# A channel mixer's memory in two pools, one of them aligned to 512 bytes, and a more urgent weight split

## The chip, the cores and the metric

The kernel runs on one core of one Trainium2 chip. The metric is the device time of one execution in microseconds (us); of several executions the median is taken. A core has a matrix engine (TensorE, PE in the profile; its weight loads are PEld), a vector engine (VectorE, DVE), a scalar engine (ScalarE, ACT), a general one (GpSimd, POOL) and a queue that issues transfers (SyncE, SP). They run side by side, each through its own list of instructions in a fixed order, and wait for each other by semaphores. They work on an on-chip memory of 128 partitions; addresses below are bytes within a partition.

## The reference

A trunk of two layers over x of 512 tokens by 1024 channels, in float32. Each layer has a token mixer and then a channel mixer, each between two RMS norms. Layer 0's token mixer is retention beside neighbourhood attention, layer 1's a bidirectional state-space scan. The channel mixer, which the change is about, is the same in both:

```python
h = rms_norm(x, g_pre)
u = depthwise_conv_centered(h @ w_up, conv_w, conv_b)   # width 3 along the tokens
g, v = split(u)                                          # 2816 channels each
x = x + rms_norm((gelu(g) * v) @ w_down, g_post)
```

## The kernel before

**Products in three parts.** A float32 operand is split into a high part (a cast, on ACT) and a low part (source less high part, on DVE): `Env.split`, lines 107 and 108. A product is then three matmuls, high by high, high by low and low by high: `Env.mm3`, lines 116 to 118. So each weight tile goes through a load (`wst`, on SP's queue), a cast to `whi` on ACT, a subtraction to `wlo` on DVE, and then TensorE.

**The channel mixer, up stage** (`ffn`). The normed tokens come in four tiles t0 to t3. Each is scaled (`xs`, line 164), turned by eight transposes (`pt`, line 173) and split into `xh`, `xl`. Weights come in units of 1024 columns. The first four units are applied to the first 256 tokens, before the last two token tiles are turned, and then to the other 256 (128x256 matmuls). Units one and two lie in `whi`/`wlo`. Units three and four lie in tiles that serve something else later: unit three as `xb1h`, `xb1l` (where the down stage's `b1h`, `b1l` will be) and unit four as `xe2` (which the profile prints as `xe`). In layer 1, whose first two units are loaded while mixer 1 still runs, the casts of units three and four are told to stand behind the second cast of token tile 1 (`behind`). The other units follow at 512 columns, then the convolution (line 398 on ACT, 399 and 400 on DVE) and the gated product `H`.

**The down stage** (`down_strassen`) forms the second product by Strassen's scheme in seven products, with sums of quarters of the weight prepared in DRAM. Its moving operands are weights, its stationary ones parts of `H`: even products take them from `b1h`, `b1l` (`ab1h`, `ab1l` in the profile), odd ones from the memory of `xh`, `xl` (`axh`, `axl`). Weights are split in `weights`; in the last product, units 4 and 5 are split into `x1` (memory of `s3`) and `x2` (memory of `e2`). Between the products stand the post-norms of token tiles (`k`, `v_m`, `x`), and the next layer's `xs`.

**What sets the order.** A scheduler lays the instructions of each engine in the order of the program, except that work inside `tc.high_priority(n)` counts as n steps more urgent and can pass other work. It also lays tiles into memory. A pool of tiles that takes space of pools that are closed has to wait, at its first write, for all that used that space. Before, the channel mixer has one pool, `ffn_c`, at 123904 to 228032. In it lie `cwt` (the convolution's weights, 704 bytes), then `H`, `b1h`, `b1l`, `e2`, `s3`, then `wx` and the `k` tiles; behind the 704 bytes each of these starts 192 bytes past a multiple of 512. In layer 1 its space covers that of mixer 1's last tiles, `e` and `m` (218624 to 228864).

Of the kernel before, what the change touches and what calls it, by code (L numbers as in the profile page):

```python
# [8 lines left out]
F32 = mybir.dt.float32  # L9
R32 = mybir.dt.float32r  # L10
# [7 lines left out]
P = 128  # L18
S = 512
# [255 lines left out]
    return out  # L275


def down_strassen(E, pool, w, ts, H, first, g_post, done):

    nc, tc = E.nc, E.tc
    lower, upper = slice(0, HW), slice(HW, S)
    A11, A21 = H[:, :HK, upper], H[:, :HK, lower]
    A12, A22 = H[:, HK:, upper], H[:, HK:, lower]
    k0 = [0]

    def stage(i, u, cols):
        st = pool.tile([P, 1024], F32, name="wx") if k0[0] % 4 == 3 else E.wst.tile([P, 1024], F32, name="wst")
        k0[0] += 1  # L290
        nc.sync.dma_start(st[:, :cols], quarters(*i)[u])
        return st[:, :cols]

    def weights(i, u, extra=None):
        cols = 1024 if u < HK // 2 else 512
        st = stage(i, u, cols)
        if extra is None:
            hi, lo = E.whi.tile([P, 1024], R32, name="whi"), E.wlo.tile([P, 1024], R32, name="wlo")
        else:
            hi, lo = extra[:, :1024], extra[:, 1024:]  # L300
        with tc.high_priority(60):
            E.split(hi[:, :cols], lo[:, :cols], st)
        return [(hi[:, c:c + 512], lo[:, c:c + 512]) for c in range(0, cols, 512)]

    a, bb = ([E.mm.tile([P, 512], F32, name="mm") for _ in range(2)] for _ in range(2))
    s3 = pool.tile([P, HK, HW], F32, name="s3")
    d = []

    def raw(i):
        tt, stt = nc.vector.tensor_tensor, nc.vector.scalar_tensor_tensor  # L310
        if i == 1:
            tt(s3, A11, A21, op=ALU.subtract)
            return s3
        if i == 2:
            tt(A21, A22, A21, op=ALU.subtract)
            stt(A11, A11, -1.0, A21, op0=ALU.mult, op1=ALU.subtract)
            return A11
        if i == 6:
            stt(A11, A12, -1.0, A11, op0=ALU.mult, op1=ALU.subtract)
            return A11  # L320
        return {3: A22, 4: A21, 5: A12}[i]

    def prepare(i):
        if i % 2:
            hi, lo = (E.res.tile([P, HK, HW], R32, name="a" + n, tag=n) for n in ("xh", "xl"))
        else:
            hi, lo = (pool.tile([P, HK, HW], R32, name="a" + n, tag=n) for n in ("b1h", "b1l"))
        src = raw(i)
        for c in (slice(0, 5), slice(5, HK)):
            E.split(hi[:, c], lo[:, c], src[:, c])  # L330
        return hi, lo

    seq = ((w, 0), a), ((ts, 1), bb), ((ts, 2), a), ((ts, 3), bb), ((ts, 0), a), ((w, 2), d), ((w, 3), a)
    kept = {}
    st = {}
    op, nxt = first, None
    started = []
    for i, (src, bank) in enumerate(seq):
        last = i == len(seq) - 1
        if not bank:  # L340
            bank.extend(E.px.tile([P, 512], F32, name="pd", tag="px") for _ in range(2))
        more = any(bank is x for x in started)
        started.append(bank)

        def mms(t, ws, u):
            for j, w_ in enumerate(ws):
                k = 2 * u + j
                cc = slice(t * P, t * P + P)
                E.mm3(bank[t], op[0][:, k, cc], op[1][:, k, cc], *w_, not more and k == 0, k == HK - 1, more)

        if last:
            ex = {4: pool.tile([P, 2048], R32, name="x1", tag="s3"), 5: pool.tile([P, 2048], R32, name="x2", tag="e2")}
            ws = [weights(src, u, ex.get(u)) for u in range(HK // 2 + 1)]
            for t in range(2):
                for u, x in enumerate(ws):
                    if (t, u) == (0, 1):
                        E.operands()
                    if u == 1:
                        E.finish(f"t{t}", st, done)
                    mms(t, x, u)  # L360
                E.post_half(st, 2 + t, 1, bank[t], g_post, sign=-1.0)
                E.finish(f"x{2 + t} s{2 + t}", st, done)
            continue
        for uu in ((0,), (1,), (2,), (3,), (4, 5)):
            ws = [(weights(src, u), u) for u in uu]
            for t in range(2):
                for x, u in ws:
                    mms(t, x, u)
            if uu == (1,):
                nxt = prepare(i + 1)  # L370
        op = nxt
        for t in range(2):
            if i in (0, 1, 2):
                kept[i, t] = pool.tile([P, 512], F32, name=f"k{i}{t}")
                nc.scalar.copy(kept[i, t], bank[t])
            else:
                j, tok, n = {3: (2, 0, 0), 4: (1, 0, 1), 5: (0, 2, 0)}[i]
                m = kept[j, t]
                nc.vector.tensor_tensor(m, bank[t], m, op=ALU.add)
                E.post_half(st, tok + t, n, m, g_post, m=m, sign=1.0 - 2 * n)  # L380
                if i == 4:
                    E.finish(f"x{t} s{t}", st, done)
    E.late += [lambda s=s: E.finish(s, st, done) for s in LATE]


def ffn(E, w_up, cw, w_down, ts, g_post_row, done, w1=None):


    nc, tc = E.nc, E.tc
    with ExitStack() as ctx:  # L390
        cp = ctx.enter_context(tc.tile_pool(name="ffn_c", bufs=1))
        cwt = cp.tile([P, 2, NF, 4], F32, name="cwt")
        H = cp.tile([P, NF, S], F32, name="H")

        def conv(ps, s, f):
            w = lambda i: cwt[:, s, f, i:i + 1]
            o = E.tmp.tile([P, S], F32, name=f"cv{s}", tag="tmp")
            nc.scalar.activation(o, ps, AF.Identity, scale=w(1), bias=w(3))  # L398
            nc.vector.scalar_tensor_tensor(o[:, 1:], ps[:, :S - 1], w(0), o[:, 1:], op0=ALU.mult, op1=ALU.add)  # L399
            nc.vector.scalar_tensor_tensor(o[:, :S - 1], ps[:, 1:], w(2), o[:, :S - 1], op0=ALU.mult, op1=ALU.add)  # L400
            return o

        def tail(f, pg, pv):
            g = conv(pg, 0, f)
            nc.scalar.activation(g, g, AF.Gelu_apprx_tanh)  # L405
            v = conv(pv, 1, f)
            nc.vector.tensor_tensor(H[:, f], g, v, op=ALU.mult)

        def extra(tags):
            t = [cp.tile([P, 2048 // len(tags)], R32, name="x" + n, tag=n) for n in tags]  # L410
            t = t if len(t) == 2 else [t[0][:, :1024], t[0][:, 1024:]]
            return [x[:, c:c + 512] for x in t for c in (0, 512)]

        u0, u1, st = w1 or (E.wunit(w_up[0, 0]), E.wunit(w_up[1, 0]), None)

        behind = E.turned[1][1] if w1 else None
        w0 = [[u0, u1], [E.wunit(w_up[0, 1], extra(("b1h", "b1l")), st, behind=behind),
                         E.wunit(w_up[1, 1], extra(("e2",)), behind=behind)]]
        nc.sync.dma_start(cwt, cw)
        p0 = [[E.mm.tile([P, S], F32, name="mm") for s in range(2)] for f in range(2)]  # L420
        for c in range(2):
            for i in range(4):
                f, s = i // 2, i % 2
                E.proj_fm(p0[f][s], w0[f][s], c * 256, c * 256 + 256)
                if c == 0 and i in (1, 2):
                    E.flush()
        for f in range(2):
            tail(f, *p0[f])
        for f in range(2, NF):
            ps = []  # L430
            for s in range(2):
                behind = w1 and f == 2
                st = E.wload(w_up[s, f], E.mid if behind and s == 0 else None)
                w = E.wunit(None, st=st, behind=E.turned[3][1] if behind else None)
                ps.append(E.mm.tile([P, S], F32, name="mm"))
                E.proj_fm(ps[-1], w)
            tail(f, *ps)
            E.chore(2)
            if f == HK + 3:
                first = [cp.tile([P, HK, HW], R32, name="a" + n, tag=n) for n in ("b1h", "b1l")]  # L440
                for k in range(0, HK, 4):
                    c = slice(k, min(k + 4, HK))
                    E.split(first[0][:, c], first[1][:, c], H[:, c, HW:])
        g_post = E.bcast(g_post_row)
        down_strassen(E, cp, w_down, ts, H, first, g_post, done)


def log1p_exp_neg(E, alloc, z):
# [884 lines left out]
```

## Time and profile before

| | |
|---|---|
| median of three runs | 1391.11 us (1390.11 to 1395.13) |
| profiled execution, its own time | 1389.62 us |
| its span | 1387.8 us |
| mean granted TensorE clock | 0.997 |

The profile is of one execution. Times in its rows are us from the start of the span, and 1.8 us lie around the span. In it layer 0's channel mixer lasts from 262 to 623 us (its down stage from 470), mixer 1 to 1026, and layer 1's channel mixer to the end. A row of the timeline gives start, duration, engine, line, operation, output and inputs; what stands in brackets is the idle time before the instruction and who ended it. A name after the arrow is an input: of a matmul first the moving operand, then the stationary one.

### The profile page before, as it was taken

What the parts mean: (1) busy time and instruction counts of PE and PEld (TensorE: products, weight loads), DVE (VectorE), ACT (ScalarE), POOL (GpSimd) and SP (SyncE); (2) the same over time, 40 slices, a digit from 0 to 9 for tenths busy, and PEclk for the clock granted to TensorE, in tenths of its full rate; (3) what the DMA queues carried; (4) which work ended last, traced back from release to release, by engine and by line L of the source; (5) the groups of instructions that cost most, each with busy time, mean ns of one, the idle gap of its engine ahead of it and who ended that gap; (6) DMA issues with size and microseconds to landing.
All of it is one profiled execution on the core that took longest, in us unless ns stands there. A gap on an engine that the chain in (4) does not pass through costs nothing.

```text
span 1387.8 us, 18078 instructions
## 1 busy us (share of the span) xinstructions
PE 1358.7 (98%) x6776; PEld 1119.8 (81%) x6776; DVE 984.4 (71%) x1402; ACT 758.2 (55%) x1233; POOL 108.9 (8%) x130
## 2 busy tenths in 40 slices
PE   7999999999999999999999999999989999999997
PEld 6877777898888888888778787777879888888886
DVE  7378888655565559797878686897886556556876
ACT  5356666443433345564978787377454434334563
POOL 0011110100011100010000010000010001110000
PEclk9999999999999999999999999999999999999999
DMA  7443232246679926653565454273434668993654
GB/s 294 146 139 107 88 90 96 69 143 238 230 204 231 227 85 198 195 190 127 159 184 181 137 183 141 68 204 117 140 126 160 218 223 225 225 221 97 196 180 142
DMA packets 69368, 229.81 MB, mean 166 GB/s; under 512 B 8352, under 2 KB 9120, under 8 KB 68768
## 3 DMA queue, kind: packets, MB, share of 16 engines
q1 hardware_dynamic: 54224, 167.30, 37.3%
q0 software_dynamic: 7168, 46.14, 13.7%
q10 hardware_dynamic: 7888, 15.21, 4.1%
q8 instruction: 54, 0.88, 0.3%
q14 instruction: 34, 0.28, 0.1%
HBM read 221.01 MB, written 51.64 MB: 196 GB/s over the span
## 4 chain that ended last, share of the span: by engine, by line
PE 85%; ACT 5%; DVE 4%; DMA 2%; issue 2%; POOL 1%; DVEq 0%; SPq 0%; POOLq 0%; ACTq 0%
PE mm L116 25%; PE mm L117 25%; PE mm L118 25%; PE pi L999 1%; PE st L948 1%; ACT pb L978 1%; DMA pb<-pd 1%; PE py L1019 1%; DMA wst<-in_c_fm 1%; PE pt L173 1%; ACT whi L107 1%; DVE wlo L108 1%; PE y L674 1%; PE pt L892 1%; PE pd L118 0%
## 5 line engine op out<-in xcount | busy, mean ns | idle before, releaser
L116 PE MATMUL mm<-xh,whi 128*128 128x512 f32 (+1 forms) x1216 | 464.0, 382 | 0.7 <-ACT z L918 0.3
L117 PE MATMUL mm<-xh,wlo 128*128 128x512 f32 (+2 forms) x1216 | 462.9, 381 | 1.1 <-DVE wlo L108 1.1
L118 PE MATMUL mm<-xl,whi 128*128 128x512 f32 (+2 forms) x1216 | 463.3, 381 | 0.5 <-DVE xl L108 0.5
L108 DVE TENSOR_TENSOR wlo<-wst,whi 128x1024 fp32r<-128x1024 f32 (+1 forms) x232 | 279.6, 1209 | 65.5 <-ACT whi L107 64.8
L107 ACT CAST whi<-wst 128x1024 fp32r<-128x1024 f32 (+1 forms) x232 | 238.4, 1032 | 102.4 <-PE mm L117 67.9
L116 PEld LDWEIGHTS mm<-xh,whi 128*128 128x128 f32 x1216 | 228.2, 188 | 45.9 <-issue 2.5
L118 PEld LDWEIGHTS mm<-xl,whi 128*128 128x128 f32 (+1 forms) x1216 | 228.0, 188 | 45.0 <-issue 1.3
L117 PEld LDWEIGHTS mm<-xh,wlo 128*128 128x128 f32 (+1 forms) x1216 | 228.3, 188 | 44.1 <-DVE wlo L108 1.5
L399 DVE SCALAR_TENSOR_TENSOR cv<-mm,cwt,cv 128x511 f32<-128x511 f32 x88 | 65.9, 749 | 182.4 <-ACT cv L398 182.4
L398 ACT ACTIVATE cv<-mm,cwt 128x512 f32<-128x512 f32 x88 | 68.6, 780 | 212.7 <-PE mm L118 212.7
L978 ACT ACTIVATE pb<-pb,tok 128x128 f32<-128x128 f32 x256 | 80.8, 392 | 8.7 <-DMA pb<-pd 7.3
L400 DVE SCALAR_TENSOR_TENSOR cv<-mm,cwt,cv 128x511 f32<-128x511 f32 x88 | 66.0, 750 | 2.8
L117 PE MATMUL mm<-whi,ab1l 128*128 128x512 f32 x164 | 64.5, 393 | 0.0
L116 PE MATMUL mm<-whi,ab1h 128*128 128x512 f32 x164 | 64.5, 393 | 0.0
L118 PE MATMUL mm<-wlo,ab1h 128*128 128x512 f32 x164 | 63.7, 389 | 0.0
L912 DVE SCALAR_TENSOR_TENSOR xf<-mm,cwt,xf 128x511 f32<-128x511 f32 (+1 forms) x64 | 47.5, 743 | 6.9 <-ACT xf L909 6.4
L274 POOL DMA_DIRECT2D ts<-in_f_down x48 | 29.9, 647 | 272.2 <-PE mm L118 267.7
L405 ACT ACTIVATE cv<-cv 128x512 f32<-128x512 f32 x44 | 27.8, 633 | 42.3 <-DVE cv L400 42.2
L116 PE MATMUL mm<-whi,yh 128*128 128x512 f32 x104 | 40.9, 395 | 1.7 <-DVE xf L912 1.7
L117 PE MATMUL mm<-whi,yl 128*128 128x512 f32 x104 | 41.1, 395 | 0.0
L1031 POOL TENSOR_TENSOR sq<-sq 128x512 f32<-128x512 f32 x11 | 16.7, 1514 | 309.9 <-ACT sq L1025 246.3
L118 PE MATMUL mm<-wlo,yh 128*128 128x512 f32 x104 | 40.6, 391 | 0.0
(308 smaller groups left out, 2120.7 us busy)
## 6 DMA issues: line engine op xcount, KB each, us to landing
wst<-in_f_up SPq DMA_DIRECT2D x88, 512.0 KB
ts<-in_f_down POOLq DMA_DIRECT2D x48, 704.0 KB, 5.8
wst<-in_c_fm SPq DMA_DIRECT2D x40, 512.0 KB
wst<-ts SPq DMA_DIRECT2D x32, 512.0 KB
pb<-pd ACTq DMA_DIRECT2D x29, 512.0 KB
wst<-in_f_down SPq DMA_DIRECT2D x24, 512.0 KB
ts<-ts POOLq DMA_DIRECT2D x16, 704.0 KB, 9.3
wst<-in_ab_fm SPq DMA_DIRECT2D x20, 512.0 KB
```

Of the source, the lines that this page charges most:

```text
L107: first = self.nc.scalar.copy(hi, src)
L108: second = self.nc.vector.tensor_tensor(lo, src, hi.bitcast(F32), op=ALU.subtract)
L116: mm(out, lh, rh, start=first, stop=False)
L117: mm(out, ll, rh, start=False, stop=False)
L118: self.product = mm(out, lh, rl, start=False, stop=last)
L274: out.append(lambda i=i, src=src, j=j, c=c, kw=kw: gp.dma_start(part(ts, i, c), part(src, j, c), **kw))
L398: nc.scalar.activation(o, ps, AF.Identity, scale=w(1), bias=w(3))
L399: nc.vector.scalar_tensor_tensor(o[:, 1:], ps[:, :S - 1], w(0), o[:, 1:], op0=ALU.mult, op1=ALU.add)
L400: nc.vector.scalar_tensor_tensor(o[:, :S - 1], ps[:, 1:], w(2), o[:, :S - 1], op0=ALU.mult, op1=ALU.add)
L405: nc.scalar.activation(g, g, AF.Gelu_apprx_tanh)
L912: nc.vector.scalar_tensor_tensor(r[:, a], ps[:, b], wc(j), r[:, a], op0=ALU.mult, op1=ALU.add)
L978: nc.scalar.activation(pb[:, dr, c], pb[:, dr, c], AF.Identity, scale=1.0 - 2 * dr, bias=tok[:, 0, c, dr * H + h:dr * H + h + 1])
```

## The change

It does three things. (1) The pool is made two: `ffn_h` holds `H`, `b1h`, `b1l`, `e2` and `s3` from 123904 to 210944, each now at a multiple of 512; `ffn_c` holds `cwt` at 210944, and `wx` and the `k` tiles where they were. The sum of both is as large as before. (2) `s3` is made in `ffn` and handed to `down_strassen`. (3) The weight splits of the down stage are made urgent by 150 steps in place of 60.

```diff
--- before.py
+++ after.py
@@ -275,7 +275,7 @@
     return out
 
 
-def down_strassen(E, pool, w, ts, H, first, g_post, done):
+def down_strassen(E, big, pool, w, ts, H, s3, first, g_post, done):
 
 
 
@@ -298,12 +298,11 @@
             hi, lo = E.whi.tile([P, 1024], R32, name="whi"), E.wlo.tile([P, 1024], R32, name="wlo")
         else:
             hi, lo = extra[:, :1024], extra[:, 1024:]
-        with tc.high_priority(60):
+        with tc.high_priority(150):
             E.split(hi[:, :cols], lo[:, :cols], st)
         return [(hi[:, c:c + 512], lo[:, c:c + 512]) for c in range(0, cols, 512)]
 
     a, bb = ([E.mm.tile([P, 512], F32, name="mm") for _ in range(2)] for _ in range(2))
-    s3 = pool.tile([P, HK, HW], F32, name="s3")
     d = []
 
     def raw(i):
@@ -324,7 +323,7 @@
         if i % 2:
             hi, lo = (E.res.tile([P, HK, HW], R32, name="a" + n, tag=n) for n in ("xh", "xl"))
         else:
-            hi, lo = (pool.tile([P, HK, HW], R32, name="a" + n, tag=n) for n in ("b1h", "b1l"))
+            hi, lo = (big.tile([P, HK, HW], R32, name="a" + n, tag=n) for n in ("b1h", "b1l"))
         src = raw(i)
         for c in (slice(0, 5), slice(5, HK)):
             E.split(hi[:, c], lo[:, c], src[:, c])
@@ -349,7 +348,7 @@
                 E.mm3(bank[t], op[0][:, k, cc], op[1][:, k, cc], *w_, not more and k == 0, k == HK - 1, more)
 
         if last:
-            ex = {4: pool.tile([P, 2048], R32, name="x1", tag="s3"), 5: pool.tile([P, 2048], R32, name="x2", tag="e2")}
+            ex = {4: big.tile([P, 2048], R32, name="x1", tag="s3"), 5: big.tile([P, 2048], R32, name="x2", tag="e2")}
             ws = [weights(src, u, ex.get(u)) for u in range(HK // 2 + 1)]
             for t in range(2):
                 for u, x in enumerate(ws):
@@ -388,9 +387,8 @@
 
     nc, tc = E.nc, E.tc
     with ExitStack() as ctx:
-        cp = ctx.enter_context(tc.tile_pool(name="ffn_c", bufs=1))
-        cwt = cp.tile([P, 2, NF, 4], F32, name="cwt")
-        H = cp.tile([P, NF, S], F32, name="H")
+        hp, cp = (ctx.enter_context(tc.tile_pool(name=n, bufs=1)) for n in ("ffn_h", "ffn_c"))
+        H = hp.tile([P, NF, S], F32, name="H")
 
         def conv(ps, s, f):
             w = lambda i: cwt[:, s, f, i:i + 1]
@@ -407,7 +405,7 @@
             nc.vector.tensor_tensor(H[:, f], g, v, op=ALU.mult)
 
         def extra(tags):
-            t = [cp.tile([P, 2048 // len(tags)], R32, name="x" + n, tag=n) for n in tags]
+            t = [hp.tile([P, 2048 // len(tags)], R32, name="x" + n, tag=n) for n in tags]
             t = t if len(t) == 2 else [t[0][:, :1024], t[0][:, 1024:]]
             return [x[:, c:c + 512] for x in t for c in (0, 512)]
 
@@ -416,6 +414,8 @@
         behind = E.turned[1][1] if w1 else None
         w0 = [[u0, u1], [E.wunit(w_up[0, 1], extra(("b1h", "b1l")), st, behind=behind),
                          E.wunit(w_up[1, 1], extra(("e2",)), behind=behind)]]
+        s3 = hp.tile([P, HK, HW], F32, name="s3")
+        cwt = cp.tile([P, 2, NF, 4], F32, name="cwt")
         nc.sync.dma_start(cwt, cw)
         p0 = [[E.mm.tile([P, S], F32, name="mm") for s in range(2)] for f in range(2)]
         for c in range(2):
@@ -437,12 +437,12 @@
             tail(f, *ps)
             E.chore(2)
             if f == HK + 3:
-                first = [cp.tile([P, HK, HW], R32, name="a" + n, tag=n) for n in ("b1h", "b1l")]
+                first = [hp.tile([P, HK, HW], R32, name="a" + n, tag=n) for n in ("b1h", "b1l")]
                 for k in range(0, HK, 4):
                     c = slice(k, min(k + 4, HK))
                     E.split(first[0][:, c], first[1][:, c], H[:, c, HW:])
         g_post = E.bcast(g_post_row)
-        down_strassen(E, cp, w_down, ts, H, first, g_post, done)
+        down_strassen(E, hp, cp, w_down, ts, H, s3, first, g_post, done)
 
 
 def log1p_exp_neg(E, alloc, z):
```

The built programs differ in these places. On ACT, at the start of layer 1's channel mixer (`xh<-pt` turns token tiles, `ssx` and `ssm` are sums of squares for the norms, `m` is a tile of mixer 1; in brackets the engines and queues that a row waits for), before:

```order
L107 CAST xh<-pt 128x4x128 [waits PE_49] x2
L153 ACTIVATE junk,ssx<-x 128x1025 [waits DVE_49,Activation_49]
L153 ACTIVATE junk,ssm_8963<-m 128x512 [waits Activation_49]
L153 ACTIVATE junk,ssm_8983<-m 128x512 [waits DVE_49,Activation_49]
L107 CAST xh<-pt 128x4x128 [waits PE_49]
L107 CAST xb1h<-wst 128x512 [waits DVE_49,DMAHW2_49,Activation_49,Pool_49]
L107 CAST xb1h<-wst 128x512
L153 ACTIVATE junk,ssx<-x 128x1025 [waits DVE_49]
L107 CAST xe_9034<-wst 128x512 [waits DMAHW4_49]
L107 CAST xe_9034<-wst 128x512
L107 CAST xh<-pt 128x4x128 [waits PE_49] x3
```

and now:

```order
L107 CAST xh<-pt 128x4x128 [waits PE_49] x2
L107 CAST xb1h<-wst 128x512 [waits DMAHW2_49,Activation_49,Pool_49]
L107 CAST xb1h<-wst 128x512
L107 CAST xe_9040<-wst 128x512 [waits DMAHW4_49]
L107 CAST xe_9040<-wst 128x512
L153 ACTIVATE junk,ssx<-x 128x1025 [waits DVE_49]
L153 ACTIVATE junk,ssm_8967<-m 128x512 [waits Activation_49]
L153 ACTIVATE junk,ssm_8987<-m 128x512 [waits DVE_49,Activation_49]
L107 CAST xh<-pt 128x4x128 [waits PE_49] x2
L153 ACTIVATE junk,ssx<-x 128x1025 [waits DVE_49,Activation_49]
L107 CAST xh<-pt 128x4x128 [waits PE_49] x2
```

The casts of `xb1h` and `xe` now stand right behind the two casts of token tile 1, ahead of the sums of squares of tile 2, and the first of them no longer waits for DVE.

On TensorE, in the same place (`pt` are the transposes of token tile 3), before:

```order
L117 MATMUL mm<-xh,xb1l 128x256
L118 MATMUL mm<-xl,xb1h 128x256
L173 MATMUL pt<-head,xs 128x128 x8
L116 MATMUL mm<-xh,xe_9034 128x256
L117 MATMUL mm<-xh,xe_9034 128x256
L118 MATMUL mm<-xl,xe_9034 128x256
```

and now, from the tenth matmul of `xe` on:

```order
L116 MATMUL mm<-xh,xe_9040 128x256
L117 MATMUL mm<-xh,xe_9040 128x256
L173 MATMUL pt<-head,xs 128x128 x4
L118 MATMUL mm<-xl,xe_9040 128x256
L116 MATMUL mm<-xh,xe_9040 128x256
L173 MATMUL pt<-head,xs 128x128 x4
L117 MATMUL mm<-xh,xe_9040 128x256
L118 MATMUL mm<-xl,xe_9040 128x256
```

The transposes stood between the last matmul of `xb1` and the first of `xe`; now eleven matmuls of `xe` come first, then four transposes, two matmuls, and the other four transposes.

On DVE, in layer 0's sixth product (bank `pd`) and on into the last, before:

```order
L108 TENSOR_TENSOR ab1l<-H,ab1h 128x1280
L164 SCALAR_TENSOR_TENSOR xs<-x,r_x,gain 128x512 x2
L139 TENSOR_SCALAR v_m<-ssm_4787,ssm_4919 128x1
L193 SCALAR_TENSOR_TENSOR k_4560<-k_4560,gain 128x512
L218 SCALAR_TENSOR_TENSOR x<-k_4672,r_m,x 128x512
L218 SCALAR_TENSOR_TENSOR x<-k_4560,r_m,x 128x512
L108 TENSOR_TENSOR wlo<-wst,whi 128x1024
L108 TENSOR_TENSOR wlo<-wx,whi 128x512
L164 SCALAR_TENSOR_TENSOR xs<-x,r_x,gain 128x512 x2
L108 TENSOR_TENSOR wlo<-wst,whi 128x1024 x2
L108 TENSOR_TENSOR ab1l<-H,ab1h 128x1536
L108 TENSOR_TENSOR wlo<-wst,whi 128x1024
```

and now:

```order
L108 TENSOR_TENSOR ab1l<-H,ab1h 128x1280
L108 TENSOR_TENSOR wlo<-wst,whi 128x1024
L108 TENSOR_TENSOR wlo<-wx,whi 128x512
L164 SCALAR_TENSOR_TENSOR xs<-x,r_x,gain 128x512 x2
L139 TENSOR_SCALAR v_m<-ssm_4790,ssm_4922 128x1
L108 TENSOR_TENSOR wlo<-wst,whi 128x1024
L193 SCALAR_TENSOR_TENSOR k_4563<-k_4563,gain 128x512
L218 SCALAR_TENSOR_TENSOR x<-k_4675,r_m,x 128x512
L218 SCALAR_TENSOR_TENSOR x<-k_4563,r_m,x 128x512
L108 TENSOR_TENSOR wlo<-wst,whi 128x1024
L108 TENSOR_TENSOR ab1l<-H,ab1h 128x1536
L108 TENSOR_TENSOR x_5058<-wst,x_5058 128x1024
```

Two splits `wlo` of the sixth product, and one behind them, have gone ahead of the post-norm of token tile 1 (`xs`, `v_m`, `k`, `x`), and the split of `x1` (`x_5058`, unit 4 of the last product) now stands ahead of the last product's units 2 and 3.

## The prediction

> **What bounds the kernel now.** I read the page first, then the waits, then TensorE's timeline at the places that the change moves, then the engines that feed it there.
>
> ```profile
> span 1387.8 us, 18078 instructions
> PE 1358.7 (98%) x6776; PEld 1119.8 (81%) x6776; DVE 984.4 (71%) x1402; ACT 758.2 (55%) x1233; POOL 108.9 (8%) x130
> PE 85%; ACT 5%; DVE 4%; DMA 2%; issue 2%; POOL 1%; DVEq 0%; SPq 0%; POOLq 0%; ACTq 0%
> ```
>
> TensorE works 98% of the span and holds 85% of the chain that ended last. The change removes no matmul, so it can win only where TensorE waits, where its clock falls, or where a matmul gets shorter. The waits of TensorE that lie at moved instructions are few:
>
> ```profile
> PE pt L173 <- DVE xs L164: 9.4, 3, 7.3
> PE mm L117 <- DVE xb1l L108: 1.3, 1, 1.3
> PE mm L116 <- ACT xb1h L107: 0.9, 1, 0.9
> PE pd L118 <- DVE wlo L108: 0.8, 1, 0.8
> ```
>
> The first row is the kernel's start (7.3) and the turning of tokens, which the change leaves. The next two are one place, the start of the second layer's channel mixer; the last is the end of the first layer's down stage.
>
> **Place 1, the start of layer 1's channel mixer.** TensorE there (start, duration, what ended the idle time before):
>
> ```profile
> 1034.52 1.04 PE L173 MATMUL pt<-head,xs 128*128 128x128 f32 x8
> 1036.48 0.38 PE L116 MATMUL mm<-xh,xb1h 128*128 128x256 f32 x1 [0.93 <-ACT xb1h L107]
> 1038.14 0.39 PE L117 MATMUL mm<-xh,xb1l 128*128 128x256 f32 x1 [1.28 <-DVE xb1l L108]
> 1040.07 0.41 PE L118 MATMUL mm<-xl,xb1h 128*128 128x256 f32 x1
> 1040.29 0.41 PE L116 MATMUL mm<-xh,xb1h 128*128 128x256 f32 x1
> 1042.50 1.03 PE L173 MATMUL pt<-head,xs 128*128 128x128 f32 x8
> 1043.29 0.36 PE L116 MATMUL mm<-xh,xe 128*128 128x256 f32 x1
> 1046.20 0.28 PE L116 MATMUL mm<-xh,whi 128*128 128x256 f32 x1
> ```
>
> TensorE waits for the first half of weight unit xb1 (0.93), then for its low part (1.28), and then matmuls start 0.22 us apart (1040.07 to 1040.29), although 24 of xe take 2.91 us in all (1043.29 to 1046.20), 0.12 each. The windows say why (busy us and instructions of PE, PEld, DVE, ACT, POOL; then the granted clock, the DMA share and GB/s):
>
> ```profile
> 1036.00:1040.00 4.00, 2.24 (x11) 2.04 (x12) 3.89 (x7) 3.42 (x7) 0.58 (x2) 0.83 0.71 207
> 1040.00:1044.00 4.00, 4.00 (x29) 4.00 (x28) 2.80 (x6) 1.05 (x3) 0.00 (x0) 0.74 0.77 268
> 1044.00:1048.00 4.00, 4.00 (x37) 4.00 (x36) 3.40 (x4) 2.21 (x3) 0.00 (x0) 1.00 0.26 93
> ```
>
> After a stretch in which PE worked 2.24 of 4 us, the clock falls to means of 0.83 and 0.74. At half speed that is 0.17 × 4 × 2 + 0.26 × 4 × 2 = 3.4 us, in which about half the work is lost: 1.7 us. So this place costs two waits and a dip. Why is xb1 late? ACT:
>
> ```profile
> 1027.24 1.32 ACT L107 CAST xh<-pt 128x512 fp32r<-128x512 f32 x2 [0.64 <-PE pt L173]
> 1031.10 1.06 ACT L153 ACTIVATE junk<-x 128x1025 bf16<-128x1025 f32 x1 [2.54 <-DVE x L218]
> 1035.81 1.14 ACT L107 CAST xb1h<-wst 128x512 fp32r<-128x512 f32 x2
> 1038.58 1.13 ACT L107 CAST xe<-wst 128x512 fp32r<-128x512 f32 x2
> ```
>
> and DVE:
>
> ```profile
> 1030.92 0.74 DVE L1084 SCALAR_TENSOR_TENSOR m<-mm,rg,x 128x512 f32<-128x512 f32 x1
> 1032.90 1.41 DVE L164 SCALAR_TENSOR_TENSOR xs<-x,r_x,gain 128x512 f32<-128x512 f32 x2 [1.24 <-POOL r_x L146]
> 1034.96 0.68 DVE L191 TENSOR_TENSOR mg<-m,gain 128x512 f32<-128x512 f32 x1
> 1036.08 1.42 DVE L218 SCALAR_TENSOR_TENSOR x<-mg,r_m,x 128x512 f32<-128x512 f32 x2 [0.43 <-POOL r_m L146]
> 1037.41 1.29 DVE L108 TENSOR_TENSOR xb1l<-wst,xb1h 128x512 fp32r<-128x512 f32 x2
> 1039.33 1.42 DVE L164 SCALAR_TENSOR_TENSOR xs<-x,r_x,gain 128x512 f32<-128x512 f32 x2
> ```
>
> The cast xb1h starts at 1035.81, right after DVE's mg ends (1034.96 + 0.68 = 1035.64), the last reader of mixer 1's tile m. The tile xb1 lies in the one pool, which takes the space of m's pool, and its first writer waits for that reader. It is not the weights: ACT, idle for 2.54 us before 1031.10, has nothing else that it could run.
>
> The change moves xb1h, xb1l, e2 and H into a large pool below m's addresses; only the small pool (cwt, wx, k) still waits for m. In the changed order ACT casts xb1h and xe right behind the two xh casts of token tile 1. These end at 1028.56; the four casts take 1.14 + 1.13, to 1030.85, inside the idle time (to 1031.10): they cost nothing while that cover lasts, with 0.25 us to spare. DVE does xb1l behind m, from 1031.66 to 1032.95, in the 1.24 us before xs: at most 0.05 us late. xe's low part stands behind the two x (1037.41) and gives its first half at 1038.1, its second at 1038.7.
>
> TensorE then: turning from 1034.52 lasts 0.79 to the next matmul (as 1042.50 to 1043.29), so xb1 starts at 1035.31. Its 24 matmuls at 0.12 end at 1038.2, just as xe's low half lands; 11 of xe follow, to 1039.5. There the changed order has token tile 3's transposes, and these wait as before: xs at 1039.33 gives its first half at 1040.05 and its second at 1040.75. Four transposes, two matmuls, four transposes (to 1041.2), then xe's last 11 (1.3): the second column half starts at 1042.5, not 1046.20. **Term 1: −3.7 us**, both waits and the dip (4.4) less a new wait of about 0.7 for xs. From 1038.2 PE is then idle 0.7 of 3, much less than in the stretch before the dip, so I count no new dip. If the timed executions had no dip to lose (it depends on where the clock's windows fall), the term is 3.7 − 1.7 = −2.0; if a dip followed the new wait, it is also −2.0. The Trainium skill ("TensorE: Matmul & The Clock Gate", Part 1: The HAM clock gate) says that the clock halves after an idle window of about 3.4 us and that the windows run free. By that rule a stretch that is more than half busy should not dip; here it did, and the 3.4 us of its length agree. Read strictly, it would leave term 1 at −2.0.
>
> **Place 2, the end of layer 0's down stage.** The priority of 150 pulls the weight splits ahead of the post-norm there.
>
> ```profile
> 602.95 0.50 PE L118 MATMUL pd<-wlo,axh 128*128 128x512 f32 x1 [0.77 <-DVE wlo L108]
> 597.76 1.42 DVE L164 SCALAR_TENSOR_TENSOR xs<-x,r_x,gain 128x512 f32<-128x512 f32 x2 [0.44 <-POOL r_x L146]
> 601.68 1.22 DVE L108 TENSOR_TENSOR wlo<-wst,whi 128x1024 fp32r<-128x1024 f32 x1
> 595.72 1.05 ACT L107 CAST whi<-wst 128x1024 fp32r<-128x1024 f32 x1
> 607.91 1.06 ACT L107 CAST whi<-wx 128x1024 fp32r<-128x1024 f32 x1 [0.27 <-DMA wx<-in_f_down]
> 609.82 1.06 ACT L107 CAST x<-wst 128x1024 fp32r<-128x1024 f32 x1
> ```
>
> The split wlo has its high part at 596.77 and runs at 601.68, behind xs, a sum and x; moved ahead of them it ends near 598.5, and the wait (0.77, and some 0.2 of the matmul behind it) goes: −1.0. The post-norm gets later by two splits, and its xs is needed only by transposes at the next product. Against it: in the last product x1, the split of weight unit 4, now stands ahead of those of units 2 and 3 on ACT and DVE. The loads start some 4 us earlier, as their buffers come free at the earlier splits; then x1's cast ends near 607.3, unit 2's at 608.3 and its low part at 609.7, when TensorE needs it. That is tight, and I charge 0.4 of the 1.0. **Term 2: −0.6** (bounds −1.0 and 0). Elsewhere (layer 1's last products, the end of the up stage, stores behind loads on SP) the splits move where TensorE waits for nothing now: zero.
>
> **Place 3, the 512-byte alignment.** The tiles H, b1h, b1l, e2 and s3 move from 192 bytes past a multiple of 512 to a multiple. No trace has both for one tile; the nearest are matmuls whose stationary operand (last name) lies one way or the other:
>
> ```profile
> L117 PE MATMUL mm<-whi,ab1l 128*128 128x512 f32 x70 | 27.6, 394 | 0.0
> L116 PE MATMUL mm<-whi,ab1h 128*128 128x512 f32 x70 | 27.5, 393 | 0.0
> L118 PE MATMUL mm<-wlo,ab1h 128*128 128x512 f32 x69 | 26.8, 388 | 0.0
> L117 PE MATMUL mm<-whi,axl 128*128 128x512 f32 x44 | 17.1, 389 | 0.0
> L117 PE MATMUL mm<-xh,wlo 128*128 128x256 f32 x32 | 9.1, 283 | 0.0
> L117 PE MATMUL mm<-xh,xb1l 128*128 128x256 f32 x16 | 4.4, 278 | 0.0
> ```
>
> ab1 lies 192 past, ax on a multiple: 393 + 394 + 388 against 3 × 389 is 8 ns a triple; with 4 products × 2 token tiles × 11 × 2 layers = 176 triples that is 1.4 us to win. In the up stage it is the other way: 278 (192 past) against 283 (on a multiple), 5 ns on two of three matmuls, 64 triples, 0.6 us to lose. I take the middle: **term 3: −0.4**, bounds −1.4 and +0.6. The splits of DVE and ACT are off the path here.
>
> **Sum:** −3.7 − 0.6 − 0.4 = −4.7 against the profiled execution's 1389.62, 1384.9. The median of the runs shown is 1.49 higher (1391.11), and the change should stand to it as the executions do: **1386.4**.
>
> **Rivals.**
> 1. Half the gain: no dip is saved, or a new one follows. −2.0 − 0.6 − 0.4 = −3.0: 1388.1. For it: the dip stood in one execution; against it: two waits so close are in every execution.
> 2. The wait is not removed: the casts stand earlier but still wait for something as late as m's reader (the xs at 1032.90 delays xb1l, or ACT is late, with only 0.25 us to spare). Then only terms 2 and 3 remain, −1.0: 1390.1. Against it: of the four engines on which the cast waited, DVE is gone from its list in the changed program.
> 3. Slower: ACT blocks at x1's cast in layer 0's last product. If its load is not earlier than now, the cast ends at 609.82 + 1.06 = 610.9 and unit 2's low part, behind one cast and two splits, at 613.2, 3.5 us late; with a dip of 1.7 that is +5.2. With terms 1 and 3 and without the gain of place 2: −3.7 − 0.4 + 5.2 = +1.1: 1392.2. It decides as soon as the load lands after about 606.3. Against it: its buffer hangs on the split of unit 0, which moves forward.
> 4. Alignment is worth more than the rows show, in LDWEIGHTS too, three times the −1.4: with −3.7 − 0.6, −8.5: 1382.6.
>
> **Chances and range.** Forecast 0.55, rival 1 0.20, rival 2 0.08, rival 3 0.06, rival 4 0.11. The range takes the bounds −3.7 − 1.0 − 1.4 = −6.1 (1385.0) and rival 1 with its bounds, −2.0 + 0 + 0.6 = −1.4 (1389.7), and on both sides 1.5 us for a median of runs that spread over 5 us: 1383.3 to 1391.2. A half percent, 7 us, is about what a measurement of this kernel can tell from no change: faster than 1384.2 needs rival 4 or the lower bound with luck, 0.13; slower than 1398.1 needs rival 3 twice over, 0.03; the same, 0.84.
>
> **What will show it.** In the changed profile: xb1h near 1028.6 after layer 1's start is lined up, no wait for xb1h or xb1l, the clock at 1.00 there, a wait of 0.6 to 0.7 at token tile 3's transposes; no wait of pd for wlo; in layer 0's last product no wait of TensorE for whi or wlo of unit 2; ab1 at 389 and xb1 at 283. I am wrong if a dip appears behind the new wait, or if x1's cast waits for its DMA with the casts of units 2 and 3 behind it.

## The result, and the profile after

| | before | changed |
|---|---|---|
| median of 13 runs | 1390.07 us (1386.69 to 1395.13) | 1386.98 us (1384.31 to 1388.42) |
| ratio | | 0.9974, 95% interval 0.9962 to 0.9986 |
| span of the profiled execution | 1387.8 us | 1383.0 us |

The ratio is 3.6 us of 1390.07, with an interval of 1.9 to 5.3. The forecast was 4.7 less, 1386.4; it lies 0.6 from the measured median, and the profiled span fell by 4.8. The sum came out, but partly by luck. The forecast counted its 4.7 from 1391.11, the median of the first three executions; the median of all thirteen is 1.0 lower, and the two medians of the table differ by 3.1. And the largest term holds in full only in executions in which the clock falls at place 1, as it did in the profile that the forecast was read from.

**Place 1.** TensorE's timeline of the changed kernel at the start of layer 1's channel mixer (start, duration, what ended the idle time before):

```profile
1033.14 1.04 PE L173 MATMUL pt<-head,xs 128*128 128x128 f32 x8
1034.07 0.36 PE L116 MATMUL mm<-xh,xb1h 128*128 128x256 f32 x1
1034.27 0.28 PE L117 MATMUL mm<-xh,xb1l 128*128 128x256 f32 x1
1037.01 0.28 PE L116 MATMUL mm<-xh,xe 128*128 128x256 f32 x1
...
1039.31 0.63 PE L173 MATMUL pt<-head,xs 128*128 128x128 f32 x4 [0.70 <-DVE xs L164]
1040.02 0.60 PE L173 MATMUL pt<-head,xs 128*128 128x128 f32 x4
1041.64 0.28 PE L118 MATMUL mm<-xl,xe 128*128 128x256 f32 x1
```

xb1's 24 matmuls run from 1034.07 to 1037.01 without a wait, and the one wait left is the forecast one, 0.70 for xs of token tile 3. The windows there (busy us of PE, PEld, DVE, ACT, POOL; clock, DMA share, GB/s) show a full clock behind it:

```profile
1034.00:1038.00 4.00, 4.00 (x34) 3.88 (x33) 3.57 (x7) 2.01 (x4) 1.08 (x2) 1.00 0.54 162
1038.00:1042.00 4.00, 3.30 (x29) 3.13 (x28) 3.70 (x6) 1.90 (x3) 0.38 (x1) 1.00 0.77 296
```

And the cause on ACT, in the same kernel:

```profile
1025.87 1.31 ACT L107 CAST xh<-pt 128x512 fp32r<-128x512 f32 x2 [0.64 <-PE pt L173]
1027.26 1.14 ACT L107 CAST xb1h<-wst 128x512 fp32r<-128x512 f32 x2
1028.30 1.13 ACT L107 CAST xe<-wst 128x512 fp32r<-128x512 f32 x2
1029.66 1.06 ACT L153 ACTIVATE junk<-x 128x1025 bf16<-128x1025 f32 x1 [0.22 <-DVE x L218]
```

The four casts fill the idle time in front of the sum of squares; 0.22 us of it is left (0.25 was forecast).

**Place 2.** The wait of pd for wlo near 603 us is gone. What is late next is at the first matmuls of mixer 1:

```profile
624.72 0.38 PE L118 MATMUL mm<-xl,whi 128*128 128x256 f32 x1 [0.47 <-DVE mean L801]
```

The row names a memset that happens to end there; the matmul reads xl, the low part of a turned token tile, which DVE gives at 623.98 + 0.69 = 624.67:

```profile
623.98 0.69 DVE L108 TENSOR_TENSOR xl<-pt,xh 128x512 fp32r<-128x512 f32 x1
```

In the kernel before, the same instruction ran 0.7 us later, and TensorE, which came to its matmul 1.2 us later there, lost only 0.1 us to it:

```profile
624.69 0.68 DVE L108 TENSOR_TENSOR xl<-pt,xh 128x512 fp32r<-128x512 f32 x1
```

**Where the time went, stage by stage.** The table gives the us between the starts of fixed matmuls in each profile: from layer 0's first xb1 matmul to its first ab1 (A), to the first pd (B), to the last product (C), to that product's last matmul (D), through mixer 1 to the turning of token tile 0 (E), to the second column half at layer 1's start (F, which holds place 1), to layer 1's first ab1 (G), and to the last ab1 of the kernel (H). From the third row on the kernels are those of the experiments.

| kernel | A | B | C | D | E | F | G | H | low clock |
|---|---|---|---|---|---|---|---|---|---|
| before | 235.43 | 75.24 | 16.03 | 16.69 | 395.77 | 27.02 | 228.81 | 105.11 | in F |
| changed | 235.84 | 74.80 | 14.96 | 16.76 | 395.86 | 23.70 | 229.15 | 104.49 | no |
| before, again | 235.43 | 75.24 | 16.02 | 16.74 | 397.32 | 25.68 | 229.08 | 105.11 | no |
| changed, again | 235.83 | 74.80 | 14.96 | 16.80 | 396.14 | 24.00 | 229.15 | 104.49 | no |
| pools alone | 235.84 | 74.80 | 16.03 | 16.57 | 398.41 | 24.07 | 229.15 | 104.49 | in E |
| urgency alone | 235.43 | 75.24 | 14.96 | 16.82 | 398.15 | 25.65 | 229.08 | 105.11 | in E |
| alignment alone | 235.84 | 74.80 | 16.03 | 16.57 | 395.69 | 27.18 | 229.15 | 104.49 | in F |
| wait put back | 235.84 | 74.80 | 14.96 | 17.53 | 395.70 | 25.12 | 229.15 | 104.49 | no |
| pools swapped | 235.43 | 75.24 | 14.96 | 17.29 | 395.87 | 25.41 | 229.08 | 105.11 | no |
| two more edits | 235.43 | 74.80 | 14.96 | 17.48 | 394.04 | 24.04 | 229.08 | 104.49 | no |
| xb1 and xe shifted | 235.43 | 74.80 | 14.96 | 16.71 | 396.75 | 24.07 | 228.82 | 104.49 | no |

The last column names the stage in which the granted clock fell to half for 3.4 us; the fall at the kernel's end, behind TensorE's last matmuls, stands in every profile and is left out. A, B, C and H repeat to 0.01 us and hang on the kernel alone. D, E, F and G vary: E, of which only the 0.4 us at mixer 1's first matmuls belongs to the change, by over 4 us. G takes one of two values, 228.8 or 229.1, where xb1 and xe lie 192 bytes past a multiple of 512, in the kernel before as in the last two of the table; what decides between them stays open. So one profile of a kernel says nothing on a difference of 2 us in the whole span, but much on one of 0.1 us in a stage that repeats.

### The profile page after: what moved, and what is told of

Same layout as the page of the kernel before. It is cut to its first block, busy times and chain, and to the rows that moved or that the text cites. A ratio compares the mean times of both kernels' runs of the same rounds, so it can differ in the third digit from the quotient of the medians.

```text
span 1383.0 us, 18079 instructions
## 1 busy us (share of the span) xinstructions
PE 1356.4 (98%) x6776; PEld 1119.3 (81%) x6776; DVE 985.0 (71%) x1402; ACT 758.2 (55%) x1233; POOL 113.6 (8%) x130
## 4 chain that ended last, share of the span: by engine, by line
PE 85%; DVE 5%; ACT 4%; DMA 2%; issue 2%; POOL 1%; SPq 0%; DVEq 0%; POOLq 0%; ACTq 0%
PE mm L116 25%; PE mm L118 25%; PE mm L117 25%; DMA pb<-pd 2%; PE pi L999 1%; PE st L948 1%; PE py L1019 1%; ACT pb L978 1%; DVE wlo L108 1%; PE pt L173 1%; PE y L674 1%; DVE xs L164 1%; PE pt L892 1%; ACT whi L107 1%; DMA wst<-in_ab_v 0%
## 5 line engine op out<-in xcount | busy, mean ns | idle before, releaser
L116 PE MATMUL mm<-whi,xh 128*128 128x512 f32 x104 | 40.7, 398 | 0.0
```

Source lines behind the costliest of these rows:

```text
L116: mm(out, lh, rh, start=first, stop=False)
```

## Experiments

**The pools alone, the urgency alone, the alignment alone.** The first is the changed kernel with 60 in place of 150:

```diff
-        with tc.high_priority(150):
+        with tc.high_priority(60):
             E.split(hi[:, :cols], lo[:, :cols], st)
```

> The two pools alone, with the down stage's splits at 60 steps as before. If the pools carry the gain: no wait of TensorE for xb1h or xb1l and no low clock at layer 1's start, the wait of pd for wlo (0.8 us near 603 us) is back, span 1383.3 to 1384.2 (before 1387.8, change 1383.0), ratio to before 0.997 to 0.998. If the urgency carries it: span near 1387, ratio 0.999 to 1.000.

Measured: 1386.63 us, ratio 0.9971 (0.9960 to 0.9982), the same as the whole change. Place 1 is as in the changed kernel (F 24.07), and the wait of pd is back:

```profile
602.59 0.50 PE L118 MATMUL pd<-wlo,axh 128*128 128x512 f32 x1 [0.78 <-DVE wlo L108]
```

The span, 1386.6, missed what was expected by 2.4 us or more, and the table shows where: E took 398.41 us. There ACT waits for a transfer of mixer 1 longer than in the kernel before, TensorE idles, and a stretch at a low clock follows. First ACT in the kernel before, then in this one:

```profile
699.35 0.40 ACT L978 ACTIVATE pb<-pb,tok 128x128 f32<-128x128 f32 x1 [2.33 <-DMA pb<-pd]
```

```profile
701.47 0.40 ACT L978 ACTIVATE pb<-pb,tok 128x128 f32<-128x128 f32 x1 [4.09 <-DMA pb<-pd]
```

and the windows of this kernel at that place:

```profile
702.00:706.00 4.00, 2.13 (x5) 1.76 (x6) 1.68 (x4) 3.99 (x7) 0.00 (x0) 0.72 1.01 227
706.00:710.00 4.00, 4.00 (x16) 3.21 (x16) 1.81 (x3) 3.98 (x12) 0.00 (x0) 0.85 0.53 126
```

This execution took 1388.37 us, the second longest of the ten; their median is 1.7 below it. So the pools carry the gain.

The second is the kernel before with 150 in place of 60 in the down stage:

> The urgency of 150 alone, with the one pool. As the step at place 2 has it: no wait of pd for wlo, TensorE 1.1 us earlier at 610 us, about 0.4 to 0.5 us of it given back at mixer 1's first matmuls because DVE is late there; the waits for xb1h and xb1l and the stretch at a low clock at layer 1's start remain. Span 1387.0 to 1387.5, ratio 0.999 to 1.0005. If the urgency carries the gain: span near 1384. If the last product loses by it: span over 1388.

Measured: 1389.87 us, ratio 0.9998 (0.9986 to 1.0009). TensorE wins 1.07 us (C, 16.03 to 14.96) and gives back 0.1 in the last product and 0.37 at mixer 1's first matmuls. That is the step as forecast, and too small for the times. The two waits of place 1 are there, 0.92 and 1.28 us, but F is 25.65, not 27.02: no low clock followed them in this execution. The span, 1387.9, came out above the 1387.0 to 1387.5 expected: E took 398.15, with a stretch at a low clock.

The third pads the small tile ahead of H in the one pool, so that no instruction moves and only addresses do:

```diff
-        cwt = cp.tile([P, 2, NF, 4], F32, name="cwt")
+        cwt = cp.tile([P, 256], F32, name="cwt")[:, :2 * NF * 4].rearrange("p (s f w) -> p s f w", s=2, f=NF)
```

> The alignment alone: one pool and 60 steps, the small tile ahead of H padded from 704 to 1024 bytes, so every instruction stands where it stood before and only addresses move. If the addresses act through the stationary operand alone: ab1 matmuls at 226 to 227 ns from start to start instead of 229 to 232 (0.6 us a layer won), xb1 and xe matmuls at 120 instead of 115 (0.45 us a layer lost), the waits at layer 1's start unchanged, span 1387.3 to 1387.8. If alignment carries more than its rows show: span under 1386.5. If it acts on casts or splits too: their mean durations change.

Measured: 1389.33 us, ratio 0.9999 (0.9987 to 1.0010). The span, 1388.0, is 0.2 above what was expected; the part ahead of A took 0.6 us longer than before (280.66 against 280.02). The addresses alone give what the rows of two different tiles had hinted. First the up stage of layer 0 (128x256), then the down stage of layer 1 (128x512), of this kernel:

```profile
L116 PE MATMUL mm<-xh,xb1h 128*128 128x256 f32 x16 | 4.6, 288 | 0.0
L118 PE MATMUL mm<-xl,xb1h 128*128 128x256 f32 x16 | 4.5, 283 | 0.0
L117 PE MATMUL mm<-xh,xb1l 128*128 128x256 f32 x16 | 4.5, 282 | 0.0
```

```profile
L116 PE MATMUL mm<-whi,ab1h 128*128 128x512 f32 x82 | 31.9, 389 | 0.0
L117 PE MATMUL mm<-whi,ab1l 128*128 128x512 f32 x82 | 31.9, 389 | 0.0
L118 PE MATMUL mm<-wlo,ab1h 128*128 128x512 f32 x82 | 31.9, 389 | 0.0
```

On a multiple of 512 bytes, ab1 goes from the 393, 394 and 388 of the prediction's rows to 389 three times, and xb1l from 278 to 282. In stages: A +0.41, B −0.44, D −0.12, H −0.62; G +0.07 against the higher of its two values, F +0.16. The sum is −0.5. ACT's cast ab1h stayed at 1.48 us for 128x1536 and DVE's ab1l at 1.75.

**The wait put back into the changed kernel.** The cast xb1h is told to stand behind mg, the last reader of mixer 1's m (the line that keeps mg is not shown):

```diff
-        w0 = [[u0, u1], [E.wunit(w_up[0, 1], extra(("b1h", "b1l")), st, behind=behind),
+        w0 = [[u0, u1], [E.wunit(w_up[0, 1], extra(("b1h", "b1l")), st, behind=E.mg if w1 else None),
```

> The change whole, aligned and urgent, but the cast xb1h is told to wait for mg, the last reader of mixer 1's tile m, as the one pool made it wait. If that wait is the cause at layer 1's start: xb1h starts after mg again, TensorE waits there 2 us or more for xb1h and xb1l, with or without a low clock behind it; span 1385.0 to 1386.8, ratio 0.998 to 0.9995. If the gain came from the addresses or from the order of the rest: span near 1383.0.

Measured: 1387.33 us, ratio 0.9985 (0.9975 to 0.9995); span 1385.2. The wait is back, but smaller than the 2 us or more expected:

```profile
1036.62 0.39 PE L116 MATMUL mm<-xh,xb1h 128*128 128x256 f32 x1 [1.24 <-ACT xb1h L107]
1036.84 0.28 PE L116 MATMUL mm<-xh,xe 128*128 128x256 f32 x1
1038.36 0.39 PE L117 MATMUL mm<-xh,xb1l 128*128 128x256 f32 x1 [0.40 <-DVE xb1l L108]
```

The scheduler knew of the wait and laid matmuls of xe, whose casts were done, between the two: 1.24 + 0.40 against 0.93 + 1.28 before. F rises from 23.7 to 24.1 to 25.12, 1.1 to 1.4 us for the wait alone. So the wait costs time whatever the addresses.

**The two pools in the other order.** The large pool above the small one, over mixer 1's m again:

```diff
-        hp, cp = (ctx.enter_context(tc.tile_pool(name=n, bufs=1)) for n in ("ffn_h", "ffn_c"))
+        cp, hp = (ctx.enter_context(tc.tile_pool(name=n, bufs=1)) for n in ("ffn_c", "ffn_h"))
```

> The two pools in the other order: the small one at 123904 and the large one above it, at 140992 to 228032, so that the large one covers mixer 1's tile m again (and lies 192 bytes past a multiple of 512); the urgency is kept. If the overlap of addresses is what made the cast wait: both waits are back, layer 1's start takes 25.6 us (27.0 with a low clock), ab1 matmuls are at 229 to 232 ns again, span near that of the urgency alone, 1385 to 1388. If having two pools is enough: 23.7 us there, span 1383 to 1386.

Measured: one run of 1387.8 us, span 1386.0. Both waits are back, 0.92 and 1.28 against 0.93 and 1.28:

```profile
1035.94 0.39 PE L116 MATMUL mm<-xh,xb1h 128*128 128x256 f32 x1 [0.92 <-ACT xb1h L107]
1037.61 0.39 PE L117 MATMUL mm<-xh,xb1l 128*128 128x256 f32 x1 [1.28 <-DVE xb1l L108]
```

Two pools are not enough; what counts is that the pool written early does not cover a tile that is read late. The tile itself need not lie there: by the sizes in the kernel `b1h`, the memory of xb1h, is at 186048 to 197312 in this kernel, and m begins at 218624. It is the pool's first write that waits. H takes 105.11 again, as in the kernel before, since the large pool is 192 bytes past a multiple of 512 again.

**Second profiles of both kernels.**

> A second profile of the kernel before, unchanged. From the turning of token tile 0 to the second column half at layer 1's start it took 27.02 us with a stretch at a low clock, and the urgent kernel with the same waits took 25.65 us without one. If the low clock comes by chance: 25.6 or 27.0, either way, with the same two waits of 0.9 and 1.3. If it belongs to the waits: 27.0 again. Mixer 1 took 395.7 to 395.9 us in four profiles and 398.2 to 398.4 in two (pools alone, urgency alone); if that too is chance, it may come at either value here.

> A second profile of the changed kernel. Stages as in the first to 0.4 us, except mixer 1 (395.9 us, or near 398.3 if that is chance) and the last product of layer 0 (16.8, or up to 17.5 if the load of x1 lands late, as in the kernel with the wait put back). Layer 1's start 23.7 to 24.1, no low clock there. Span 1383 to 1386.

The kernel before, again: one run of 1390.62 us, F 25.68. The same two waits (0.92 and 1.27), and a full clock behind them:

```profile
1038.00:1042.00 4.00, 1.92 (x14) 1.72 (x15) 3.56 (x6) 3.36 (x8) 0.91 (x2) 1.00 0.67 173
1042.00:1046.00 4.00, 4.00 (x37) 4.00 (x36) 4.00 (x7) 2.56 (x6) 0.00 (x0) 1.00 0.79 267
```

Of the five profiles with the waits in this order (before twice, urgency, alignment, swapped pools), the low clock follows in two, and what it costs is 27.02 − 25.68 = 1.3 us.

The traces show what decides. In a profile that has two falls of the clock, one in the kernel and one at its end, they lie a whole number of 3.413 us apart: 1038.63 and 1383.37 are 101 of these windows apart in the kernel before, 703.80 and 1383.05 are 199 with the pools alone. Counted back by such windows from the fall at the end, the window ahead of the low clock in the kernel before, and that window itself, are:

```profile
1035.22:1038.63 3.41, 1.20 (x9) 0.77 (x7) 2.98 (x6) 2.77 (x6) 0.82 (x1) 1.00 0.47 125
1038.63:1042.04 3.41, 3.41 (x19) 3.41 (x18) 3.37 (x7) 1.55 (x4) 0.54 (x1) 0.50 0.93 344
```

In the second profile, whose clock falls at 1386.80 at the end, the same counting (102 windows) parts the waits: most of the first (its idle time runs from 1037.89 to 1038.81) falls into one window, its rest and the second into the next:

```profile
1035.24:1038.65 3.41, 2.64 (x23) 2.40 (x21) 2.98 (x6) 1.92 (x5) 0.92 (x1) 1.00 0.19 68
1038.65:1042.06 3.41, 1.98 (x14) 1.78 (x15) 3.37 (x6) 2.83 (x7) 0.55 (x1) 1.00 0.81 210
```

TensorE was busy 1.20 us in the one window that holds both waits, and 2.64 and 1.98 us in the two over which they are spread. The other three low stretches inside a kernel follow windows with 0.70, 1.08 and 1.19 us. Over all eleven profiles, from 15 us on, every window in which PE was busy 1.42 us or less was followed by the half clock, and none with 1.59 or more. So the waits are the same in each execution, and where the windows lie, which differs between executions, decides whether the clock falls. By sliding such a window over TensorE's rows at layer 1's start, an estimate: with the two waits in this order 40 to 46% of its positions hold less than 1.5 us of work, in the changed kernel none does (never under 1.99).

The changed kernel, again: one run of 1385.62 us, span 1383.8, F 24.00, E 396.14, each within what was expected.

**Two attempts at more.** The first takes the last product out of the urgency and shifts xb1 and xe 192 bytes off the multiple of 512, with ab1 left on it (xe moves to the memory of s3, which has the room):

```diff
-        with tc.high_priority(150):
+        with tc.high_priority(60 if i == (w, 3) else 150):
...
-            t = [hp.tile([P, 2048 // len(tags)], R32, name="x" + n, tag=n) for n in tags]
+            t = [hp.tile([P, 2048 // len(tags) + 48], R32, name="x" + n, tag=n)[:, 48:] for n in tags]
...
-                         E.wunit(w_up[1, 1], extra(("e2",)), behind=behind)]]
+                         E.wunit(w_up[1, 1], extra(("s3",)), behind=behind)]]
```

> The changed kernel with two edits: xb1 and xe lie 192 bytes past a multiple of 512 again while ab1 stays on one, and the last product's splits go back to 60 steps. If the stationary operand's address alone sets the pace: xb1 and xe at 113 to 118 ns instead of 120, 0.4 us a layer won, ab1 still at 226 to 227. If the last product's urgency is what gives back 0.4 us at mixer 1's first matmuls: no wait of TensorE for mean or xl at 624 us, 0.4 won. Together span 1.0 to 1.3 us below the changed kernel's in equal stages; the timed ratio to before 0.9965, within the interval of the changed kernel's.

Measured: 1386.77 us, ratio 0.9979 (0.9969 to 0.9989). The shift did what was expected (A 235.43 again with H at 104.49). The other half was wrong: the wait at mixer 1's first matmuls is still there with 0.27, and the last product takes 17.48, since DVE now does the post-norm before unit 2's low part, for which TensorE waits:

```profile
610.60 0.50 PE L118 MATMUL mm<-wlo,ab1h 128*128 128x512 f32 x1 [0.60 <-DVE wlo L108]
```

So the second attempt keeps the urgency and only shifts:

> The changed kernel, urgency of the last product kept at 150, with xb1 and xe 192 bytes past a multiple of 512 and ab1 on one. By the stages so far: layer 0's up stage 235.43 instead of 235.84 us, ab1 at 226 to 227 ns, the stage from the second column half at layer 1's start 229.08 instead of 229.15; layer 1's start itself unchanged at 23.7 to 24.1, because TensorE waits there for token tile 3 and shorter matmuls only make that wait longer. 0.5 us below the changed kernel in equal stages, which the times cannot show: ratio to before 0.996 to 0.998. If the address has nothing to do with it, 235.84 stays.

Measured: 1386.50 us, ratio 0.9968 (0.9955 to 0.9981). A falls by 0.41 against the changed kernel, as expected. G falls by 0.33 where 0.07 was expected; it took the lower of its two values. F does not fall (24.07), as expected: there the shorter matmuls only lengthen the wait for token tile 3. By its stages without E this is the quickest of the kernels, by 0.4 us against the first profile of the changed kernel and 0.7 against the second; the times cannot tell it from the changed one.

## Why the prediction was right, and where it was not

**Term 1, −3.7: the mechanism right, the size too large where the clock does not fall.** The pair of profiles gives F 27.02 to 23.70, −3.3. The missing 0.4 comes from a step that the forecast put at almost nothing: xb1l in DVE's idle time ahead of xs, "at most 0.05 us late". POOL's r_x of token tile 2, for which xs waits, runs at the same time, and it took 0.46 longer than before; DVE, free at 1031.49, began xs at 1031.93. Before, and changed:

```profile
1032.33 0.54 POOL L146 TENSOR_TENSOR r_x<-ssx,head 128x1 f32<-128x1 f32 x1 [3.45 <-ACT junk L153]
```

```profile
1030.89 1.00 POOL L146 TENSOR_TENSOR r_x<-ssx,head 128x1 f32<-128x1 f32 x1 [3.38 <-ACT junk L153]
```

In all five profiles of this order (changed twice, pools alone, both attempts at more) r_x takes 1.00 us and ends 0.40 after the end of xb1l. That POOL's instruction waits for DVE's is what these rows suggest; no run tested it.

But −3.3 holds only where the low clock follows the waits. Without it the same step is 25.68 to between 23.70 and 24.07: −1.6 to −2.0, which is the −2.0 of rival 1. The forecast took the dip of one execution for part of the place and argued against rival 1 that the two waits are in every execution. They are; the dip is not. Nor is its 4.4 for both waits and the dip their sum, 0.93 + 1.28 + 1.7 = 3.9; it is the −3.7 of the whole place with the 0.7 of the new wait added back. How many of the timed executions had the dip is known in part: of the 60 of the kernel before that were timed beside the experiments 34 show a mean of 0.997 or less, as the four profiles with a low stretch inside the kernel do, and of the 14 of the changed kernel one. Mixer 1 can add such a stretch too, so the share that belongs to place 1 stays open. That no new dip follows the new wait was right. The Trainium skill ("TensorE: Matmul & The Clock Gate", Part 1: The HAM clock gate) says that the windows run free, and the runs agree: the same waits meet a low clock or do not. Its other half, that an idle window is needed, does not fit: PE was busy 0.70 to 1.20 of the 3.41 us ahead of each low stretch inside a kernel. The 2.24 of 4 us from which the forecast reasoned ran past the fall at 1038.63.

That the wait is one of address overlap, and not of two pools or of the order, is shown by the swapped pools; that it is the wait that costs the time, by the wait put back.

**Term 2, −0.6: the size about right, the reason half wrong.** The stall removed is 1.07, in every urgent kernel. The 0.4 to be given back was charged to unit 2's low part in the last product. In the changed kernel's two profiles TensorE did not wait there; it gave back 0.2 in the product (D 16.76 and 16.80 against 16.57 in the two kernels with the same addresses and 60 steps) and 0.42 to 0.47 at mixer 1's first xl, a place the forecast did not name. Moved post-norms were said to be needed only later: DVE has them in the last product instead, and its chain from there to mixer 1 gains 0.7 us where TensorE gains 1.2 (in both figures 0.2 lies ahead of the channel mixer). I have not settled which of DVE's instructions holds that chain; taking the last product's urgency away did not free it.

**Rival 3 was real, and small.** Where x1's load lands late, ACT blocks and unit 2 behind it. ACT and TensorE in the kernel with the wait put back:

```profile
607.06 1.05 ACT L107 CAST x<-wst 128x1024 fp32r<-128x1024 f32 x1 [1.16 <-DMA wst<-in_f_down]
```

```profile
610.55 0.51 PE L118 MATMUL mm<-wlo,ab1h 128*128 128x512 f32 x1 [0.66 <-DVE wlo L108]
```

and in the one with the pools swapped:

```profile
606.66 1.05 ACT L107 CAST x<-wst 128x1024 fp32r<-128x1024 f32 x1 [0.87 <-DMA wst<-in_f_down]
```

```profile
610.16 0.50 PE L118 MATMUL mm<-wlo,ab1h 128*128 128x512 f32 x1 [0.34 <-DVE wlo L108]
```

A load that landed at 607.06 lost TensorE 0.66 us, one that landed at 606.66 lost it 0.34. Both put the point from which it decides at 606.3 to 606.4; the forecast said 606.3. In the changed kernel x1's cast began at 605.60. The 3.5 us that the rival would have cost needed a load as late as before, and none was. But in these two of the six profiles with 150 steps in the last product, D is 0.5 to 0.8 longer than in the others, which is about what the urgency wins; what made the load land late stays open.

**Term 3, −0.4: right,** −0.5 by the kernel in which only addresses moved, with the sign and nearly the size of each half as the rows of before had it (ab1 −1.2 over B, D and H, where −1.4 was worked out; the up stages +0.6).

**The sum.** Without a low clock in F the terms are −1.8, −0.5 and −0.5, −2.8; with one, −4.1 to −4.3. The timed difference of 3.6 lies between, and its interval (1.9 to 5.3) holds both; with the dip in 40 to 46% of the executions the terms would give −3.3 to −3.4, an estimate. Rivals 2 and 4 fell: xb1h no longer waits, and the alignment is worth no more than its rows. A slip of no weight: the lower bound of the range, 1385.0 less 1.5, is 1383.5 and not 1383.3.

## What to carry to other kernels

A pool that is written early should not cover the space of a tile that is read late; a second pool helps only if it moves that overlap. Before a stretch at a low clock is counted as part of a stall, a second profile of the same kernel should show it again, and TensorE's work should be read in the 3.41 us just ahead of the fall and not in windows of one's own choice. Where the total wanders by more than the change is worth, the time between the starts of two fixed matmuls, stage by stage and in several profiles, tells which part did what.

## What the hardware showed that was not expected

- The start of a stationary operand changes a matmul's length, and the sign depends on the width; one offset, 192 bytes, was tried. At 128x512, 388 to 394 ns at 192 bytes past a multiple of 512 against 389 on it; at 128x256, 278 to 283 against 282 to 288. The shifted kernel holds both in one: ab1 at 389, xb1l at 278.
- Four of eleven profiles have a low clock inside the kernel, twice in mixer 1 and twice at layer 1's start, for 3.41 us each time. It follows a window of 3.41 us in which TensorE was busy 0.70 to 1.20 us; it needs no idle window. Over all profiles 1.42 us were too little and 1.59 enough.
- Beside DVE's xb1l, POOL's r_x took 1.00 us in place of 0.54 and ended 0.40 behind it, in each of the five profiles in which the two stand side by side.
- Mixer 1 took 394.04 to 398.41 us in kernels whose edits lie elsewhere; one transfer of pb, waited for 2.33 us in one and 4.09 in another, is part of it. What sets that transfer's time stays open.
